# Ones-matrix products in a rounded format, and a last output block in two halves of 256 tokens

## The chip, the cores and the metric

The kernel runs on one core of one Trainium2 chip. The metric is device time in microseconds, from the first to the last instruction of the program and what lies around it. Five engines matter: TensorE (PE in the profile, its weight loads PEld), VectorE (DVE), ScalarE (ACT), GpSimd (POOL) and SyncE (SP), whose queue issues most of the transfers.

## What is computed

A trunk of two layers on 2048 tokens with 1024 channels, all float32:

```
h = rms_norm(x, norm_w);  proj = h @ w_in
branch A: gated delta rule, 4 heads, chunks, forward and backward, summed
branch B: u = cf_val * sigmoid(cf_glu); u = depthwise_conv31(u) + b
          u = silu(layer_norm(u, cf_ln_w, cf_ln_b)); y_b = (u * silu(z_b)) @ w_cf_out
y = gate_a * y_a + gate_b * y_b
x = x + y @ w_out
```

and after the second layer one more `rms_norm(x, final_norm_w)`. The change touches the norms (one value per token, which has to reach all 128 channels of a tile) and the very last output product.

## The kernel before, in words

Activations lie with channels on the 128 partitions and tokens along the free axis. A dense product of full precision is made of three products in a rounded format (`F32R`): the weight is split into a high part `whi` and a low part `wlo`, the activation into `hi` and `lo`, and for each block of 128 input channels `dense_steps` (L174 to L176) runs whi x hi, whi x lo and wlo x hi with 512 tokens moving. `split` (L157, L158) makes the two parts: ScalarE copies to the rounded format, VectorE subtracts. `weight` loads a tile of 128 output channels by two transfers of 256 KB each through two load buffers (`wraw`), and splits into a ring of two `whi` and two `wlo`.

A norm has three steps that use a 128x128 matrix of ones or the identity. `token_sum` (L200) sums squares over the channels by a product with one column of ones and leaves one sum per token, with the tokens on partitions. `rsqrt` (L190 to L196) makes the inverse root on VectorE by eleven short operations. `spread` takes these values back to a row that stands on all partitions: for each group of 128 tokens it scales the identity by the column (L206, VectorE) and multiplies by the ones (L208, TensorE), in full precision, four times for 512 tokens. Its users are the first norm (four blocks), the layer norm of branch B (`conformer_norm`, four blocks a layer), `normalise` between the layers (four) and `last_out` (four). The layer norm also needs a mean: `t` holds the sum of four channel tiles, and one product with the ones in full precision (L760) sums it over partitions. In the trace a product in full precision is two instructions.

The small temporaries come from `st`, a ring of three buffers of 512 columns. The gate evacuations (L808, `go`) use the same ring: ScalarE moves a finished tile from a TensorE bank to it, and a transfer issued by ScalarE stores it. There are three banks for dense products (`pd`) and five for the rest (`pz`).

Order of work: the convolutions and norms are Python generators that `pump` runs between dense products on credit. Each `yield` names a cost; a `yield 0.0` ends the pump of this product, so that the next step comes at least one product later; `Z` says how many such stops follow each step of the layer norm. The layer norms run during the 32 tiles of `gates(0)`. After that comes `delta`, whose instructions keep their written order, with the second half of the gates as filler. Everywhere else the framework's scheduler orders each engine's instructions by priority and by when its model has them ready, so a spread stands among the next tiles' products.

`last_out` (from L1280) ends the trunk. For each half of 1024 tokens and each block of 512 it runs eight output tiles: the product, the residual row `xr` loaded and added (L1295), the square and its sum (L222, L225, L226). Then come the token sums, the inverse root (from L1303), the spread, and eight scaled outputs (L1308), each stored by SyncE or ScalarE in turn (L1311).

Of the kernel before, what the change touches and what calls it, by code (L numbers as in the profile page):

```python
# [6 lines left out]
F32 = mybir.dt.float32  # L7
# [23 lines left out]
STEP = (5, 4, 4, 4)  # L31
TAIL = (3, 3, 3)
Z = '121'
LATE = 4
AHEAD = 4
R2 = 3.7
# [25 lines left out]
def cut(x):  # L62
    return x.rearrange("p (a i) -> p a i", a=2)
# [13 lines left out]
class Trunk:  # L77
# [79 lines left out]
        self.nc.scalar.activation(hi, src, AF.Copy)  # L157
        self.nc.vector.tensor_tensor(out=lo, in0=src, in1=hi.bitcast(F32), op=ALU.subtract)  # L158
# [39 lines left out]
    def token_sum(self, ps, src, n):  # L198
        for i in range(n):
            self.nc.tensor.matmul(ps[:, i:i + 1], src[:, i * P:(i + 1) * P], self.ones[:, 0:1],  # L200
                                  start=True, stop=True)

    def spread(self, ps, r, n):
        dg = self.pst.tile([P, NB], F32, tag="st", name="dg").rearrange("p (a b) -> p a b", b=P)
        for i in range(n):
            self.nc.vector.tensor_scalar(out=dg[:, i, :], in0=self.ident, scalar1=r[:, i:i + 1],  # L206
                                         scalar2=None, op0=ALU.mult)
            self.nc.tensor.matmul(ps[:, i * P:(i + 1) * P], self.ones, dg[:, i, :], start=True, stop=True)  # L208

    def norm_stats(self, ss):  # L210
        ps = self.pz()
# [8 lines left out]
    def add_square(self, ss, x, first):  # L220
        if first:
            self.nc.scalar.activation(ss, x, AF.Square)  # L222
        else:
            sq = self.st("sq")
            self.nc.scalar.activation(sq, x, AF.Square)  # L225
            self.nc.vector.tensor_tensor(out=ss, in0=ss, in1=sq, op=ALU.add)  # L226

# [20 lines left out]
    def run(self):  # L248
        tc, nc, a = self.tc, self.nc, self.a
        with tc.tile_pool(name="cst", bufs=1) as cst, \  # L250
                tc.tile_pool(name="vec", bufs=1) as self.pv, \
                tc.tile_pool(name="dsc", bufs=1) as self.pds, \
                tc.tile_pool(name="big", bufs=4) as self.pbig, \
                tc.tile_pool(name="mid", bufs=3) as self.pmid, \
                tc.tile_pool(name="hmd", bufs=5) as self.phm, \
                tc.tile_pool(name="stg", bufs=3) as self.pst, \
                tc.tile_pool(name="sml", bufs=14) as self.psm, \
                tc.tile_pool(name="wgt", bufs=2) as self.pw, \
                tc.tile_pool(name="drm", bufs=1, space=DRAM) as drm, \
                tc.tile_pool(name="pdn", bufs=3, space=PSUM) as self.ppd, \  # L260
                tc.tile_pool(name="pzz", bufs=5, space=PSUM) as self.ppz:
            con = cst.tile([P, 4, P], F32, name="con")
            nc.scalar.dma_start(con, a["consts"])
            self.ident = con[:, C_ID, :]
            self.ones = con[:, C_ONE, :]
# [477 lines left out]
    def conformer_norm(self, blk):  # L743
        nc = self.nc
        v_ = nc.vector
        sl = slice(blk * NB, (blk + 1) * NB)
        cv = self.mid("lnc")[:, 0:L].rearrange("p (j t) -> p j t", t=NB)
        self.load(cv, self.cv_d[:, :, sl].rearrange("j p t -> p j t"))
        zb = self.mid("lnz")[:, 0:L].rearrange("p (j t) -> p j t", t=NB)
        self.load(zb, self.zb_d[:, :, sl].rearrange("j p t -> p j t"))  # L750
        t = self.st("lnt")
        s2 = self.st("lns")
        v_.tensor_tensor(out=t, in0=cv[:, 0, :], in1=cv[:, 1, :], op=ALU.add)
        v_.tensor_tensor(out=s2, in0=cv[:, 2, :], in1=cv[:, 3, :], op=ALU.add)
        v_.tensor_tensor(out=t, in0=t, in1=s2, op=ALU.add)
        yield 1.8
        for _ in range(int(Z[0])):
            yield 0.0
        ps = self.pz()
        nc.tensor.matmul(ps, self.ones, t, start=True, stop=True)  # L760
# [25 lines left out]
        v_.tensor_tensor(out=cv, in0=cv, in1=zb, op=ALU.mult)  # L786
        self.pstore(self.u_d[:, :, sl].rearrange("j p t -> p j t"), cv)
# [492 lines left out]
    def last_out(self, l, half, xd, fnw, yhi, ylo, ahead):  # L1280
        nc, a = self.nc, self.a
        v_ = nc.vector
        for b in range(2):
            sl = slice(b * NB, (b + 1) * NB)
            tk = slice(half * HALF + b * NB, half * HALF + (b + 1) * NB)
# [3 lines left out]
            for j in range(KD):  # L1289
                next(ahead, None)  # L1290
                ps = self.pd()
                self.dense(ps, w, lambda k: (yhi[:, k, sl], ylo[:, k, sl]), KD)
                xr = self.st("xr")
                self.load(xr, xd[j][:, tk])
                v_.tensor_tensor(out=cut(xn[j]), in0=sort(ps), in1=cut(xr), op=ALU.add)  # L1295
                self.add_square(ss, xn[j], j == 0)
                if j + 1 < KD:
                    w = self.weight(a["w_out"][l, j + 1], KD)
            ps = self.pz()
            self.token_sum(ps, ss, 4)  # L1300
            v = self.sm(4, "nv")
            r = self.sm(4, "nr")
            v_.tensor_scalar(out=v, in0=ps[:, 0:4], scalar1=1.0 / D, scalar2=EPS, op0=ALU.mult, op1=ALU.add)  # L1303
            self.rsqrt(r, v, 4)
            pr = self.pz()
            self.spread(pr, r, 4)
            for j in range(KD):
                v_.scalar_tensor_tensor(out=xn[j], in0=xn[j], scalar=fnw[:, j:j + 1], in1=pr,  # L1308
                                        op0=ALU.mult, op1=ALU.mult)
                eng = nc.scalar if j % 2 else nc.sync  # L1310
                eng.dma_start(a["out"][j, :, tk], xn[j])  # L1311


def layout(inputs, depth):
# [49 lines left out]
```

## Time and profile before

| | us |
|---|---|
| median of 3 runs | 3219.36 |
| lowest, highest | 3217.04, 3219.66 |
| profiled execution | 3223.96 |
| its span | 3222.2 |

The span goes from the first to the last instruction of the profiled execution. In the lines of a timeline the first number is the start in microseconds from the span's start, the second the length of the merged row, then engine, line, operation, what it writes and reads, shape and count; in brackets the idle time of the engine before it and what ended that. In a row of a group there stand the busy time in all, the mean length of one in ns, and idle time with its releaser. A TensorE row's length includes the drain; the distance between starts tells what it holds the engine for.

### The profile page before, as it was taken

What the parts mean: (1) busy time and instruction counts of PE and PEld (TensorE: products, weight loads), DVE (VectorE), ACT (ScalarE), POOL (GpSimd) and SP (SyncE); (2) the same over time, 40 slices, a digit from 0 to 9 for tenths busy, and PEclk for the clock granted to TensorE, in tenths of its full rate; (3) what the DMA queues carried; (4) which work ended last, traced back from release to release, by engine and by line L of the source; (5) the groups of instructions that cost most, each with busy time, mean ns of one, the idle gap of its engine ahead of it and who ended that gap; (6) DMA issues with size and microseconds to landing.
All of it is one profiled execution on the core that took longest, in us unless ns stands there. A gap on an engine that the chain in (4) does not pass through costs nothing. (4 is left out here: it accounts for less than half of the span.)

```text
span 3222.2 us, 51090 instructions
## 1 busy us (share of the span) xinstructions
PE 3101.0 (96%) x19110; PEld 2711.5 (84%) x19110; DVE 2401.9 (75%) x4409; ACT 1393.5 (43%) x3104; POOL 302.2 (9%) x297
## 2 busy tenths in 40 slices
PE   6999999999999999799999999999999999989997
PEld 5788888888889998687888888888888999877786
DVE  7789898987555687645666989898955567867655
ACT  5625252522344466533345242425234445655332
POOL 3000000000022231000000000000002122200000
PEclk9999999999999999899999999999999999999999
DMA  4233232334687785654413131314358777856644
GB/s 139 88 96 94 84 100 78 102 108 132 215 289 231 261 270 174 191 187 128 141 50 107 66 116 62 119 59 122 116 188 269 236 254 246 265 155 208 206 128 147
DMA packets 427030, 501.67 MB, mean 156 GB/s; under 512 B 95712, under 2 KB 260192, under 8 KB 426784
## 3 DMA queue, kind: packets, MB, share of 16 engines
q1 hardware_dynamic: 354032, 388.58, 38.9%
q10 hardware_dynamic: 64688, 80.09, 7.1%
q0 software_dynamic: 8064, 29.76, 2.4%
q8 instruction: 150, 2.46, 0.3%
q14 instruction: 96, 0.79, 0.1%
HBM read 342.74 MB, written 155.58 MB: 155 GB/s over the span
## 5 line engine op out<-in xcount | busy, mean ns | idle before, releaser
L174 PE MATMUL pd<-h,whi 128*128 128x512 f32 x2816 | 1091.7, 388 | 0.0
L176 PE MATMUL pd<-h,wlo 128*128 128x512 f32 x2816 | 1071.3, 380 | 2.3 <-DVE wlo L158 2.3
L175 PE MATMUL pd<-h,whi 128*128 128x512 f32 x2816 | 1072.1, 381 | 0.0
L728 DVE SCALAR_TENSOR_TENSOR cacc<-gp,vec,cacc 128x1009 f32<-128x1009 f32 (+1 forms) x480 | 615.5, 1282 | 37.8 <-ACT cacc L726 34.7
L174 PEld LDWEIGHTS pd<-h,whi 128*128 128x128 f32 x2816 | 534.6, 190 | 79.3 <-issue 1.4
L176 PEld LDWEIGHTS pd<-h,wlo 128*128 128x128 f32 x2816 | 534.4, 190 | 79.5 <-DVE wlo L158 3.9
L175 PEld LDWEIGHTS pd<-h,whi 128*128 128x128 f32 x2816 | 534.5, 190 | 72.9 <-issue 1.9
L157 ACT ACTIVATE whi<-wraw 128x512 fp32r<-128x512 f32 x400 | 243.0, 624 | 488.6 <-PE pd L175 346.6
L158 DVE TENSOR_TENSOR wlo<-wraw,whi 128x512 fp32r<-128x512 f32 x400 | 279.7, 713 | 175.8 <-ACT whi L157 163.9
L553 DVE SCALAR_TENSOR_TENSOR acc<-cin,vec,acc 128x1022 f32<-128x1022 f32 (+1 forms) x192 | 246.9, 1300 | 14.7 <-ACT acc L551 13.6
L176 PE MATMUL pd<-yhi,wlo 128*128 128x512 f32 x512 | 195.3, 381 | 8.0 <-DVE wlo L158 7.9
L174 PE MATMUL pd<-yhi,whi 128*128 128x512 f32 x512 | 194.7, 380 | 1.4 <-ACT whi L157 1.3
L175 PE MATMUL pd<-ylo,whi 128*128 128x512 f32 x512 | 194.0, 379 | 0.0
L808 ACT ACTIVATE go<-pd,vec 128x512 f32<-128x512 f32 x128 | 87.0, 680 | 133.2 <-PE pd L176 122.6
L529 ACT ACTIVATE cin<-pd 128x512 f32<-128x512 f32 x96 | 57.0, 593 | 156.3 <-PE pd L176 156.1
L174 PE MATMUL pd<-gop,whi 128*128 128x512 f32 x256 | 99.9, 392 | 20.5 <-ACT gop L157 19.3
L176 PEld LDWEIGHTS pd<-yhi,wlo 128*128 128x128 f32 x512 | 96.7, 189 | 25.6 <-DVE wlo L158 12.2
L174 PE MATMUL pd<-uop,whi 128*128 128x512 f32 x256 | 102.9, 402 | 12.8 <-ACT uop L157 7.1
L1210 ACT ACTIVATE gt<-gt 128x1024 f32<-128x1024 f32 x64 | 67.6, 1058 | 108.1 <-DMA gt<-gt 98.9
L740 ACT ACTIVATE ao<-pd 128x512 f32<-128x512 f32 x64 | 38.3, 598 | 170.0 <-PE pd L176 169.9
L976 ACT ACTIVATE dm<-pz,eg 128x128 f32<-128x128 f32 x240 | 68.5, 368 | 98.8 <-PE pz L970 93.7
L174 PEld LDWEIGHTS pd<-yhi,whi 128*128 128x128 f32 x512 | 96.8, 189 | 16.4 <-ACT whi L157 3.0
(296 smaller groups left out, 4837.0 us busy)
## 6 DMA issues: line engine op xcount, KB each, us to landing
wraw<-w_in SPq DMA_DIRECT2D x240, 256.0 KB, 3.2
gt<-go ACTq DMA_DIRECT2D x128, 256.0 KB, 3.4
dl<-gr SPq DMA_DIRECT2D x128, 256.0 KB, 5.1
dl<-kq SPq DMA_DIRECT2D x64, 512.0 KB, 5.9
dl<-kv SPq DMA_DIRECT2D x64, 512.0 KB, 5.2
gt<-gt SPq DMA_DIRECT2D x64, 512.0 KB, 5.0
wraw<-w_out SPq DMA_DIRECT2D x96, 256.0 KB, 3.0
kq<-acc SPq DMA_DIRECT2D x16, 1024.0 KB, 5.5
```

The costliest lines, as they stand in the source:

```text
L157: self.nc.scalar.activation(hi, src, AF.Copy)
L158: self.nc.vector.tensor_tensor(out=lo, in0=src, in1=hi.bitcast(F32), op=ALU.subtract)
L174: mm(ps, whi[:, k, :], xhi, start=k == 0, stop=False)
L175: mm(ps, whi[:, k, :], xlo, start=False, stop=False)
L176: mm(ps, wlo[:, k, :], xhi, start=False, stop=k == kk - 1)
L529: nc.scalar.activation(cut(t[:, o + b * NB:o + (b + 1) * NB]), sort(ps), AF.Copy)
L553: self.nc.vector.scalar_tensor_tensor(out=out, in0=t[:, k:k + n], scalar=wc(k), in1=out, op0=ALU.mult, op1=ALU.add)
L728: self.nc.vector.scalar_tensor_tensor(out=acc, in0=t[:, k:k + n], scalar=wc(k), in1=acc, op0=ALU.mult, op1=ALU.add)
L740: nc.scalar.activation(cut(o), sort(ps), func)
L808: nc.scalar.activation(cut(o), sort(ps), AF.Identity, bias=self.vec[:, V_GB + j:V_GB + j + 1])
L976: nc.scalar.activation(hv(o1)[:, hd, :], pq[:, hd, :], AF.Copy, scale=eg[:, hd:hd + 1])
L1210: nc.scalar.activation(gt, gt, AF.Sigmoid)
```

## The change

It has three parts.

The ones become a tile of their own in the rounded format (`ones_r`), loaded by a separate transfer and copied by ScalarE; the old name is a view of it. `spread` splits its column of values into a high and a low part, makes two sets of scaled identities (the high ones on VectorE, the low ones on ScalarE, each in a buffer of the `st` ring) and runs two products of up to 512 columns in the rounded format that add up in one bank.

The layer norm mean splits `t` into two buffers of the `st` ring and runs two rounded products. The squares go to fresh buffers. The step's cost for `pump` is 2.5 instead of 1.8.

In the last block of the last half, only five output tiles (`PART`) run on 512 tokens. The weights of the other three are kept in a large buffer of their own; then the three tiles run on the first 256 tokens, that half is closed (sums, inverse root, spread, outputs), and the three tiles run on the other 256 tokens, which are closed in turn. In a half the last tile's squares aren't added to the sum on VectorE, but enter the token sums as a second set of products (`token_add`).

```diff
-    def weight(self, src, kk):
-        hi = self.pw.tile([P, KD, P], F32R, tag="whi", bufs=2, name="whi")[:, 0:kk, :]
-        lo = self.pw.tile([P, KD, P], F32R, tag="wlo", bufs=2, name="wlo")[:, 0:kk, :]
+    def weight(self, src, kk, kept=None):
+        if kept:
+            hi, lo = kept
...
+    def token_add(self, ps, src, n, first, last):
+        for i in range(n):
+            self.nc.tensor.matmul(ps[:, i:i + 1], src[:, i * P:(i + 1) * P], self.ones[:, 0:1],
+                                  start=first and i == 0, stop=last, skip_group_check=True)
+
     def spread(self, ps, r, n):
-        dg = self.pst.tile([P, NB], F32, tag="st", name="dg").rearrange("p (a b) -> p a b", b=P)
+        nc = self.nc
+        rh = self.psm.tile([P, 8], F32R, tag="smr", bufs=2, name="rh")
+        self.split(rh[:, 0:n], rh[:, n:2 * n], r)
+        rh = rh.bitcast(F32)
+        dg = [self.pst.tile([P, NB], F32R, tag="st", name=f"dg{i}").rearrange("p (a b) -> p a b", b=P) for i in range(2)]
         for i in range(n):
-            self.nc.vector.tensor_scalar(out=dg[:, i, :], in0=self.ident, scalar1=r[:, i:i + 1],
-                                         scalar2=None, op0=ALU.mult)
-            self.nc.tensor.matmul(ps[:, i * P:(i + 1) * P], self.ones, dg[:, i, :], start=True, stop=True)
+            nc.vector.tensor_scalar(out=dg[0][:, i, :], in0=self.ident, scalar1=rh[:, i:i + 1],
+                                    scalar2=None, op0=ALU.mult)
+            nc.scalar.activation(dg[1][:, i, :], self.ident, AF.Copy, scale=rh[:, n + i:n + i + 1])
+        for i in range(2):
+            nc.tensor.matmul(ps[:, 0:n * P], self.ones_r, dg[i][:, 0:n, :], start=i == 0, stop=i == 1)
...
+        hi = self.pst.tile([P, NB], F32R, tag="st", name="lnh")
+        lo = self.pst.tile([P, NB], F32R, tag="st", name="lnl")
+        self.split(hi, lo, t)
+        yield 2.5
...
-        nc.tensor.matmul(ps, self.ones, t, start=True, stop=True)
+        for i, part in enumerate((hi, lo)):
+            nc.tensor.matmul(ps, self.ones_r, part, start=i == 0, stop=i == 1)
+        t = self.st("lnq")
+        s2 = self.st("lnr")
...
+            whole = PART if half and b else KD
+            if whole < KD:
+                hold = self.big([P, 2, KD, NB], F32R, "wend").rearrange("p a b c -> p (a b c)")
+                parts = [hold[:, i * D:(i + 1) * D].rearrange("p (k c) -> p k c", c=P) for i in range(2 * (KD - whole))]
...
+            ws = [self.weight(a["w_out"][l, j], KD, parts[2 * (j - whole):2 * (j - whole) + 2]) for j in range(whole, KD)]
+            n = NB // 2
+            for g in (o, o + n):
+                for j, w in zip(range(whole, KD), ws):
+                    x = product(j, w, g, n)
+                    if j + 1 < KD:
+                        self.add_square(ss[:, g % NB:g % NB + n], x, False)
+                sq = self.st("sq")[:, 0:n]
+                nc.scalar.activation(sq, x, AF.Square)
+                close(g, n, sq)
```

`product` and `close` hold the same statements as the loop of `last_out` before, with a width of 512 or 256 tokens.

More of the change, by code (lines that the diff above doesn't have):

```diff
@@ L33 @@
 Z = '121'
+PART = 5
 LATE = 4
@@ L158, in split @@
         self.nc.vector.tensor_tensor(out=lo, in0=src, in1=hi.bitcast(F32), op=ALU.subtract)
-    def weight(self, src, kk):
-        hi = self.pw.tile([P, KD, P], F32R, tag="whi", bufs=2, name="whi")[:, 0:kk, :]
-        lo = self.pw.tile([P, KD, P], F32R, tag="wlo", bufs=2, name="wlo")[:, 0:kk, :]
+    def weight(self, src, kk, kept=None):
+        if kept:
+            hi, lo = kept
+        else:
+            hi = self.pw.tile([P, KD, P], F32R, tag="whi", bufs=2, name="whi")[:, 0:kk, :]
+            lo = self.pw.tile([P, KD, P], F32R, tag="wlo", bufs=2, name="wlo")[:, 0:kk, :]
         for k in range(0, kk, 4):
@@ L223, in add_square @@
         else:
-            sq = self.st("sq")
+            sq = self.st("sq")[:, 0:x.shape[1]]
             self.nc.scalar.activation(sq, x, AF.Square)
@@ L261, in run @@
                 tc.tile_pool(name="pzz", bufs=5, space=PSUM) as self.ppz:
-            con = cst.tile([P, 4, P], F32, name="con")
-            nc.scalar.dma_start(con, a["consts"])
+            con = cst.tile([P, 3, P], F32, name="con")
+            nc.scalar.dma_start(con, a["consts"][:, 0:3])
+            ones = self.st("ones")[:, 0:P]
+            nc.scalar.dma_start(ones, a["consts"][:, C_ONE])
+            self.ones_r = cst.tile([P, P], F32R, name="ones")
+            nc.scalar.activation(self.ones_r, ones, AF.Copy)
             self.ident = con[:, C_ID, :]
-            self.ones = con[:, C_ONE, :]
+            self.ones = self.ones_r.bitcast(F32)
             self.con = con
@@ L1282, in last_out, with product, close @@
         v_ = nc.vector
+        def product(j, w, o, n):
+            sl = slice(o, o + n)
+            ps = self.pd()[:, 0:n]
+            self.dense(ps, w, lambda k: (yhi[:, k, sl], ylo[:, k, sl]), KD)
+            xr = self.st("xr")[:, 0:n]
+            self.load(xr, xd[j][:, half * HALF + o:half * HALF + o + n])
+            x = xn[j][:, o % NB:o % NB + n]
+            v_.tensor_tensor(out=cut(x), in0=sort(ps), in1=cut(xr), op=ALU.add)
+            return x
+        def close(o, n, sq):
+            q = n // P
+            c = slice(o % NB, o % NB + n)
+            ps = self.pz()
+            self.token_add(ps, ss[:, c], q, True, sq is None)
+            if sq is not None:
+                self.token_add(ps, sq, q, False, True)
+            v = self.sm(q, "nv")
+            r = self.sm(q, "nr")
+            v_.tensor_scalar(out=v, in0=ps[:, 0:q], scalar1=1.0 / D, scalar2=EPS, op0=ALU.mult, op1=ALU.add)
+            self.rsqrt(r, v, q)
+            pr = self.pz()[:, 0:n]
+            self.spread(pr, r, q)
+            for j in range(KD):
+                x = xn[j][:, c]
+                v_.scalar_tensor_tensor(out=x, in0=x, scalar=fnw[:, j:j + 1], in1=pr, op0=ALU.mult, op1=ALU.mult)
+                eng = nc.scalar if j % 2 else nc.sync
+                eng.dma_start(a["out"][j, :, half * HALF + o:half * HALF + o + n], x)
@@ L1288, in last_out @@
             w = self.weight(a["w_out"][l, 0], KD)
-            for j in range(KD):
+            for j in range(whole):
                 next(ahead, None)
[L1291 to L1297, printed above, removed]
-                    w = self.weight(a["w_out"][l, j + 1], KD)
@@ L1299, in last_out @@
[L1299 to L1311, printed above, removed]
+                x = product(j, w, o, NB)
@@ new lines, in last_out @@
+                self.add_square(ss, x, j == 0)
+                if j + 1 < whole:
+                    w = self.weight(a["w_out"][l, j + 1], KD)
+            if whole == KD:
+                close(o, NB, None)
+                continue
+            ws = [self.weight(a["w_out"][l, j], KD, parts[2 * (j - whole):2 * (j - whole) + 2]) for j in range(whole, KD)]
[8 more added lines that the diff above has]
+                close(g, n, sq)
```

4 lines of the change are left out of this document (1 added, 3 removed).

## The prediction

> **What bounds the kernel now.** I read the page first, then a table of busy time by stage.
>
> ```profile
> span 3222.2 us, 51090 instructions
> PE 3101.0 (96%) x19110; PEld 2711.5 (84%) x19110; DVE 2401.9 (75%) x4409; ACT 1393.5 (43%) x3104; POOL 302.2 (9%) x297
> 80.00:1500.00 1420.00, 1379.80 (x8766) 1212.07 (x8765) 1076.23 (x1981) 621.44 (x1431) 140.04 (x138) 0.99 0.50 158
> 2900.00:3222.00 322.00, 292.67 (x1346) 247.22 (x1344) 204.31 (x360) 120.73 (x180) 0.00 (x0) 0.98 0.53 172
> ```
>
> The columns of the last two lines are stretch, length, then PE, PEld, DVE, ACT and POOL busy, granted clock, DMA share and GB/s. PE works for 97% of the long middle at a clock of 0.99. There, PE time saved is time saved, as long as no other engine makes PE wait. In the last 322 us PE works for 91%: chains through VectorE and ScalarE show.
>
> The change concerns two products with the matrix of ones: the layer norm mean (L760, 8 times) and the spread (L208, 20 times). Their rows in the timeline of PE:
>
> ```profile
> 777.42 1.02 PE L760 MATMUL pz<-lnt,con 128*128 128x512 f32 x2
> 777.88 0.78 PE L174 MATMUL pd<-h,whi 128*128 128x512 f32 x1
> 778.49 0.38 PE L175 MATMUL pd<-h,whi 128*128 128x512 f32 x1
> 778.71 0.38 PE L176 MATMUL pd<-h,wlo 128*128 128x512 f32 x1
> 794.71 1.05 PE L208 MATMUL pz<-dg,con 128*128 128x128 f32 x8
> 795.52 0.46 PE L174 MATMUL pd<-h,whi 128*128 128x512 f32 x1
> 795.82 0.38 PE L175 MATMUL pd<-h,whi 128*128 128x512 f32 x1
> ```
>
> A product in the rounded format with 512 columns starts every 0.22 us (778.49 to 778.71). From L760's start to L175 lie 1.07 us; less the one L174 between, the mean costs PE 0.85. In the same way four spreads cost 1.11 - 0.22 = 0.89, which is 0.11 for each of eight instructions, weight load and 128 columns of full precision. Both groups are queued straight behind dense products: PE waits for neither.
>
> **The change part by part.** *Layer norm.* The mean becomes two rounded products of 512 columns, 0.43 instead of 0.85: 8 x 0.42 = 3.4 us less. The spread becomes two also, 0.43 instead of 0.89: 8 x 0.46 = 3.7 less. What it adds must hide:
>
> ```profile
> 768.63 0.69 DVE L755 TENSOR_TENSOR lnt<-lnt,lns 128x512 f32<-128x512 f32 x1
> 788.84 0.69 ACT L808 ACTIVATE go<-pd,vec 128x512 f32<-128x512 f32 x1 [3.01 <-PE pd L176]
> 791.95 0.88 DVE L206 TENSOR_SCALAR dg<-con,lr 128x128 f32<-128x128 f32 x4
> 794.69 1.15 ACT L157 ACTIVATE whi<-wraw 128x512 fp32r<-128x512 f32 x2 [5.17 <-PE pd L175]
> 778.88 0.69 ACT L808 ACTIVATE go<-pd,vec 128x512 f32<-128x512 f32 x1 [2.71 <-DMA gt<-go]
> 774.96 0.69 ACT L808 ACTIVATE go<-pd,vec 128x512 f32<-128x512 f32 x1 [0.64 <-DMA gt<-go]
> L157 ACT ACTIVATE whi<-wraw 128x512 fp32r<-128x512 f32 x400 | 243.0, 624 | 488.6 <-PE pd L175 346.6
> L1210 ACT ACTIVATE gt<-gt 128x1024 f32<-128x1024 f32 x64 | 67.6, 1058 | 108.1 <-DMA gt<-gt 98.9
> ```
>
> Before the mean, one split of 512 columns: 0.62 on ScalarE and 0.69 on VectorE, 1.4 with their hand-over. The sum was ready at 769.3 and the mean ran at 777.4, so 8 us cover it. Before the spread, a split of four columns (about 0.2 on each engine, the cost of the short operations in the rows of the end below; 0.5 in all), then four scaled identities on ScalarE beside VectorE's. Between 512 and 1024 columns ScalarE's time grows by 0.43, so 128 columns take about 0.31, and, overlapping like the pair at 794.69, four take 1.0. The operand, ready at 792.8 now, comes 0.6 to 1.2 us later, by how far the parts overlap; the spread ran at 794.7, so 1.9 us cover it. ScalarE is free from 789.5 to 794.7. If that cover goes, PE stands at the spread, and with it every gate product behind it, and each evacuation that waits for those.
>
> The cost I cannot read off is buffers: the staging ring has three, spread now takes two of them and the mean briefly three, and the gate evacuations use the same ring. Two rows show an evacuation waiting for one, 2.71 and 0.64; PE does not stop, since it has three banks. Bounds: 0, and 8 x 2.71 = 21.7. I take the shorter wait once or so a layer, +1.3, as PE rode over the longer one. The mean's larger price in the planner (2.5 for 1.8) moves the norms by one gate tile; counted through the credits, the last ends three tiles ahead of the delta stage instead of four, so the fillers stay in place. Zero.
>
> *Spreads of the norms.* Layer 0's normalise has four, in pairs between dense products: 4 x 0.46 = 1.8 less. The first norm has four more:
>
> ```profile
> PE pz L200 <- DMA x<-x: 13.6, 1, 13.6
> PE pz L208 <- DVE dg L206: 7.6, 5, 2.6
> ```
>
> In these rows of the waits PE starts by standing 13.6 us for the input, which hides the ones' own small load and ScalarE copy, and the five waits for a spread's identities fall into two spreads of the first norm, one transition and the closing spread. I count zero: -1.8 if all four are kept, +1 if two chains are longer by 0.5.
>
> *Last norm, three spreads ahead of the end.* Here VectorE's chain decides:
>
> ```profile
> 3163.84 0.17 DVE L196 SCALAR_TENSOR_TENSOR nr<-rst,nr 128x4 f32<-128x4 f32 x1
> 3164.03 0.87 DVE L206 TENSOR_SCALAR dg<-con,nr 128x128 f32<-128x128 f32 x4
> 3164.32 1.15 ACT L157 ACTIVATE whi<-wraw 128x512 fp32r<-128x512 f32 x2 [4.67 <-PE pd L175]
> 3165.57 5.36 DVE L1308 SCALAR_TENSOR_TENSOR xl<-xl,fnw,pz 128x512 f32<-128x512 f32 x8 [0.67 <-PE pz L208]
> 3172.78 0.48 PE L176 MATMUL pd<-yhi,wlo 128*128 128x512 f32 x1 [1.42 <-DVE wlo L158]
> ```
>
> From the inverse root (3164.0) to L1308 pass 1.57 us, and the 5.36 us of L1308 hold back the weight split on which PE then stands for 1.42. With the split of four columns, ScalarE's 1.0 and two products with their drain the 1.57 becomes about 2.1. PE is 0.46 earlier, its weight 0.5 later: +0.5 for each of three, +1.5. Bounds: -1.4 (PE decides), and +5 (ScalarE's identities stand behind the pair at 3164.32, 1.15 more each).
>
> *The end.* The chain after the last product, and the weights ahead of it:
>
> ```profile
> 3204.56 0.38 PE L176 MATMUL pd<-yhi,wlo 128*128 128x512 f32 x1
> 3204.97 0.69 DVE L1295 TENSOR_TENSOR xl<-pd,xr 128x512 f32<-128x512 f32 x1 [3.04 <-PE pd L176]
> 3205.75 0.63 ACT L225 ACTIVATE sq<-xl 128x512 f32<-128x512 f32 x1 [4.54 <-DVE xl L1295]
> 3206.41 0.69 DVE L226 TENSOR_TENSOR ss<-ss,sq 128x512 f32<-128x512 f32 x1 [0.74 <-ACT sq L225]
> 3207.16 1.05 PE L200 MATMUL pz<-con,ss 128*128 128x1 f32 x8 [2.22 <-DVE ss L226]
> 3208.25 0.16 DVE L1303 TENSOR_SCALAR nv<-pz 128x4 f32<-128x4 f32 x1 [1.15 <-PE pz L200]
> 3210.49 0.87 DVE L206 TENSOR_SCALAR dg<-con,nr 128x128 f32<-128x128 f32 x4
> 3212.95 5.35 DVE L1308 SCALAR_TENSOR_TENSOR xl<-xl,fnw,pz 128x512 f32<-128x512 f32 x8 [1.58 <-PE pz L208]
> 3187.06 0.63 ACT L157 ACTIVATE whi<-wraw 128x512 fp32r<-128x512 f32 x1 [2.88 <-DMA wraw<-w_out]
> 3191.18 0.64 ACT L157 ACTIVATE whi<-wraw 128x512 fp32r<-128x512 f32 x1 [1.87 <-DMA wraw<-w_out]
> 3197.07 0.69 DVE L158 TENSOR_TENSOR wlo<-wraw,whi 128x512 fp32r<-128x512 f32 x1 [0.63 <-ACT whi L157]
> L206 DVE TENSOR_SCALAR dg<-con,lr 128x128 f32<-128x128 f32 x32 | 7.1, 282 | 0.5
> ```
>
> Now: add, square, sum, token sums and their drain to 3208.25, inverse root to 3210.49, spread to 3212.95, L1308 to 3218.3, the last store 3.9 more: 17.3 us after the product's end at 3204.94. With 256 columns a VectorE operation takes about 0.42 (a third of the way from 0.28 at 128 to 0.69), a ScalarE one 0.41, eight L1308 8 x 0.40. After: add 0.45, square 0.5, token sums by four instructions 0.65, inverse root 2.24, spread 1.7, L1308 3.2, the store 3.5 (half the bytes): 12.2. That is 5.0 less.
>
> Against it, PE ends later. Six half products of 24 at 0.11 (a full weight load for 256 columns, like a spread's instruction) are 16.0 instead of 15.5; twelve more token-sum instructions and one more spread 1.5; and the weights: they come every 4.1 us (3187.06, 3191.18) by two load buffers, the last split ends at 3197.76, while the first halves want all three weights by 3197.4 at the latest, ten instructions before their end: 1.5 more. Their loads now stand on SP's queue ahead of the residual loads of the same tiles, which are needed only at a product's end. The first half's closing runs on VectorE beside the second half's products; its stores, half of them on ScalarE's queue, hold the second half's squares there until about 3208, when the last product is still running. Together 3.5 later, 5.0 shorter: -1.5 (from -5 to +2).
>
> A rule speaks against the halves. The Trainium skill, TensorE: Matmul & The Clock Gate, Part 3, section The mechanism, says that weight loads overlap with running products only where the row groups differ. By that a half product would pay its load in full, and the sum would be the last rival's; the 0.11 per instruction of the spreads at 794.71, loads included, does not agree.
>
> *Sum:* -3.4 - 3.7 + 1.3 - 1.8 + 1.5 - 1.5 = -7.6. The profiled execution took 3223.96 (span 3222.2), 0.14% above the median 3219.36; I carry the difference over: 3211.8 us.
>
> **Rivals.** *All of it kept:* the three transitions follow PE (-1.4), no buffer wait, second-half products fill the weight wait at the end (-3.0): -3.4 - 3.7 - 1.8 - 1.4 - 3.0 = -13.3, 3206.1. For it: no product of the norms waits in the rows above. Against: the 1.42 behind L1308.
>
> *Swallowed:* each of the eight means and eight spreads meets the 0.64 wait on the ring, 10.2 in place of 1.3: +1.3, 3220.7. For it: the ring was already full at 774.96. Against: two such waits in that stretch did not stop PE.
>
> *Slower, buffers:* in each of the eight norms an evacuation holds ScalarE by the 2.71 of the row at 778.88 just ahead of its half of the spread, and PE stands: 21.7 in place of 1.3 gives +12.8, 3232.2. It decides once that hold exceeds the 0.7 us of cover that the spread has left at the least (1.9 less 1.2).
>
> *Half products without overlap:*
>
> ```profile
> 777.85 0.19 PEld L174 LDWEIGHTS pd<-h,whi 128*128 128x128 f32 x1 [0.24 <-issue]
> ```
>
> If this 0.19 did not hide behind 256 columns, 144 instructions would take 27 us more, 3239. The spreads' pace speaks against it. It is the rule of the Trainium skill named above.
>
> **How the numbers follow.** Forecast 0.47, all kept 0.18, swallowed 0.20, buffers 0.12, no overlap 0.03. The forecast's own range is 3207 to 3217, mostly from the transitions and the end. The range for 8 in 10 is 3205 to 3222: it takes in both neighbours and leaves out the slower rivals. A measurement of this kernel tells about 0.2%, 6.4 us, from no change: faster means below 3212.9. The forecast lies just under it, so 0.6 of its chance and all of "all kept" count as faster, 0.46; the rest of it and "swallowed" as the same, 0.39; the two others as slower, 0.15.
>
> **What would show it.** Right: the mean and the spread as two rows of 512 columns that hold PE for 0.43; no new wait of PE on ScalarE's identities between 760 and 890; L1308 of the three transitions about 0.5 later after the inverse root; PE's last product about 3.5 us later relative to the block's start, and 12.2 us from it to the end. Wrong: PE waiting at L760 or the spread by a microsecond or more in the gates stage, half products pacing well over 0.11, a closing chain over 14 us, or other stages moving because the order of instructions changed.

## The result, and the profile after

The changed kernel takes 3267.15 us (median of 4 runs, 3265.03 to 3269.88) where the kernel before took 3218.20 beside it (3216.25 to 3219.66): a ratio of 1.0153, interval 1.0135 to 1.0171. It is 49 us slower. 3211.8 was forecast, and 3267 lies outside the range and past the dearest rival.

The page of the changed kernel begins:

```profile
span 3264.9 us, 51212 instructions
PE 3109.3 (95%) x19072; PEld 2711.7 (83%) x19072; DVE 2412.6 (74%) x4462; ACT 1428.2 (44%) x3217; POOL 303.4 (9%) x297
```

PE is busy for 8 us more and the span is 43 us longer: TensorE did not get more work, it stands. To find where, I cut both spans at the same events: the stretch from a layer's first gate evacuation (`go`, L808 before, L833 after) to its first product of `delta`, which holds the four layer norms, for both layers; and the last block's products from the first to the last. The table of busy time by stage, columns as in the prediction, for the kernel before:

```profile
715.50:904.00 188.50, 184.96 (x878) 160.20 (x879) 119.23 (x200) 65.00 (x111) 13.64 (x15) 0.99 0.56 188
2292.90:2478.30 185.40, 183.21 (x877) 158.95 (x878) 120.70 (x200) 65.04 (x111) 13.54 (x15) 1.00 0.58 191
2930.60:3204.50 273.90, 260.88 (x1200) 220.36 (x1199) 167.31 (x289) 99.65 (x151) 0.00 (x0) 1.00 0.53 173
```

and for the changed kernel:

```profile
715.70:921.80 206.10, 189.28 (x850) 162.43 (x849) 123.26 (x207) 73.92 (x135) 12.87 (x14) 0.95 0.51 170
2303.00:2510.10 207.10, 190.25 (x850) 163.52 (x851) 123.67 (x208) 73.76 (x135) 12.68 (x14) 0.94 0.50 166
2965.40:3247.80 282.40, 264.54 (x1265) 223.85 (x1263) 172.49 (x317) 104.73 (x171) 0.00 (x0) 0.99 0.52 170
```

The layer norm stretches are 17.6 and 21.7 longer, 39.3 of the 42.7 us between the spans. The last products are 8.5 longer; what lies between the stretches makes up the rest (-7.7 between the two norm stretches, +3.0 ahead of the last products, -0.6 behind them, +0.2 ahead of all). The granted clock fell from 0.99 and 1.00 to 0.95 and 0.94 in the norm stretches, and in the last products only from 1.00 to 0.99.

What TensorE waits for, by the view of waits (the row of the spread before stands in the prediction); the columns are us in all, times, longest. Before:

```profile
PE pz L200 <- DVE lnt L766: 5.7, 4, 2.0
```

After:

```profile
PE pz L204 <- DVE lnq L791: 32.2, 6, 5.7
PE pz L223 <- DVE dg L219: 11.2, 8, 4.1
```

The token sums of six of the eight norms stand for over 5 us each until VectorE has added the squares. Of the spread's 11.2 us only 0.2 lie in the two norm stretches. VectorE is not the cause. ScalarE's timeline at the first of the six:

```profile
809.01 0.69 ACT L833 ACTIVATE go<-pd,vec 128x512 f32<-128x512 f32 x1 [1.39 <-DVE lnl L159]
809.73 0.33 ACTq L152 DMA_DIRECT2D gt<-go  x1
811.90 0.63 ACT L788 ACTIVATE lnq<-lnc 128x512 f32<-128x512 f32 x1 [2.20 <-DVE lnc L786]
812.44 0.61 ACT L790 ACTIVATE lnr<-lnc 128x512 f32<-128x512 f32 x1
818.25 0.69 ACT L833 ACTIVATE go<-pd,vec 128x512 f32<-128x512 f32 x1 [5.20 <-DMA gt<-go]
819.39 0.63 ACT L790 ACTIVATE lnr<-lnc 128x512 f32<-128x512 f32 x1 [0.45 <-ACT go L833]
```

Of four squares two are done at 813.05. The third, at 819.39, could have run from 813.8 on, when VectorE's first sum (813.08, 0.69 long) had freed its buffer, but ahead of it in ScalarE's order stands a gate evacuation, which waits 5.20 us for a buffer of the staging ring: the three hold `lnq`, `lnr` and the `go` of 809.01, whose store, issued at 809.73, ends that wait. In the five other norms the evacuation at the same step waits 5.08 to 5.63. VectorE's timeline shows the sum of squares behind it:

```profile
820.05 0.69 DVE L791 TENSOR_TENSOR lnq<-lnq,lnr 128x512 f32<-128x512 f32 x1 [6.28 <-ACT lnr L790]
```

and TensorE's, first at a norm without the wait, the token sums that stand ahead of its next dense products:

```profile
793.69 0.95 PE L204 MATMUL pz<-ones,lnq 128*128 128x1 f32 x8
794.50 0.46 PE L178 MATMUL pd<-h,whi 128*128 128x512 f32 x1
...
822.19 1.87 PE L204 MATMUL pz<-ones,lnq 128*128 128x1 f32 x8 [5.31 <-DVE lnq L791]
823.92 0.77 PE L178 MATMUL pd<-h,whi 128*128 128x512 f32 x1
824.48 0.63 PE L179 MATMUL pd<-h,whi 128*128 128x512 f32 x1
...
827.90 0.47 PE L178 MATMUL pd<-h,whi 128*128 128x512 f32 x1
```

A stall costs more than itself. The token sums take 1.73 us (822.19 to 823.92) where those of the first norm took 0.81 (793.69 to 794.50). Then eight products start 0.43 apart (824.48 to 827.90) instead of 0.22, and 0.56 passes ahead of them instead of 0.22: 2.0 more. So one stall adds 0.9 + 2.0 = 2.9 of slow clock. The granted clock was 0.50 from 822.19 to 828.00. Worked out in the same way, the six stalls add 2.4 to 3.9 each, 2.9 in the mean.

The sum over both layers: token sums wait 32.2 - 5.7 = 26.5 longer; six times 2.9 is 17.4; the shorter means and spreads give back 8 x 0.81 = 6.5 (0.39 each for the mean, 0.42 for the spread, rows below). That makes 37.4 of the 39.3 measured. The rest, and slow stretches that the kernel before has too, I have not assigned.

The Trainium skill, TensorE: Matmul & The Clock Gate, Part 1, What's actually happening, says that the array drops to half its clock after an idle window of about 3.4 us and gets the full one back after as long a busy one. The stall of 5.31 agrees, and the slow stretch behind it, 5.7 us from 822.19 to 827.90, is longer than the page's window. But half pace can follow a shorter wait, as TensorE's timeline of the kernel before shows:

```profile
862.70 1.05 PE L200 MATMUL pz<-con,lnt 128*128 128x1 f32 x8 [1.54 <-DVE lnt L766]
...
864.93 0.63 PE L176 MATMUL pd<-h,wlo 128*128 128x512 f32 x1
...
867.92 0.43 PE L174 MATMUL pd<-h,whi 128*128 128x512 f32 x1
```

After a wait of 1.54 us the token sums and four products run at full pace, and then seven products take 2.99 (864.93 to 867.92), 0.43 each; the granted clock was 0.51 from 864.60 to 868.10. The three other waits for token sums in that kernel (2.00, 0.60 and 1.59) have no such stretch behind them, so these traces give no length of wait from which it comes.

In ScalarE's own waits there is one row for this ring. Before:

```profile
ACT go L808 <- DMA gt<-go: 6.7, 3, 3.3
```

After:

```profile
ACT go L833 <- DMA gt<-go: 47.8, 14, 5.6
```

### The profile page after: what moved, and what is told of

It reads as the page before. It is cut to its first block, busy times and chain, and to the rows that moved or that the text cites. A ratio compares the mean times of both kernels' runs of the same rounds, so it can differ in the third digit from the quotient of the medians.

```text
span 3264.9 us, 51212 instructions
## 1 busy us (share of the span) xinstructions
PE 3109.3 (95%) x19072; PEld 2711.7 (83%) x19072; DVE 2412.6 (74%) x4462; ACT 1428.2 (44%) x3217; POOL 303.4 (9%) x297
## 5 line engine op out<-in xcount | busy, mean ns | idle before, releaser
L159 DVE TENSOR_TENSOR wlo<-wraw,whi 128x512 fp32r<-128x512 f32 x394 | 273.0, 706 | 160.5 <-ACT whi L158 141.3
L180 PE MATMUL pd<-yhi,wlo 128*128 128x512 f32 x488 | 186.8, 383 | 9.4 <-DVE wlo L159 9.3
L178 PE MATMUL pd<-yhi,whi 128*128 128x512 f32 x488 | 186.2, 382 | 2.5 <-ACT whi L158 2.5
L179 PE MATMUL pd<-ylo,whi 128*128 128x512 f32 x488 | 185.7, 380 | 0.0
L833 ACT ACTIVATE go<-pd,vec 128x512 f32<-128x512 f32 x128 | 87.4, 683 | 163.6 <-PE pd L180 102.8
L178 PE MATMUL pd<-uop,whi 128*128 128x512 f32 x256 | 102.4, 400 | 12.2 <-ACT uop L158 7.2
L178 PEld LDWEIGHTS pd<-yhi,whi 128*128 128x128 f32 x488 | 92.7, 190 | 17.4 <-ACT whi L158 4.6
```

What stands on the lines that cost most here:

```text
L178: mm(ps, whi[:, k, :], xhi, start=k == 0, stop=False)
L179: mm(ps, whi[:, k, :], xlo, start=False, stop=False)
L180: mm(ps, wlo[:, k, :], xhi, start=False, stop=k == kk - 1)
L833: nc.scalar.activation(cut(o), sort(ps), AF.Identity, bias=self.vec[:, V_GB + j:V_GB + j + 1])
```

## The experiments

The theory to test: the mean's two parts and the fresh buffers for the squares fill the ring, an evacuation between the squares waits for a store, and the token sums wait for that. Rivals: the step cost of 2.5 only moved the norm under a badly placed evacuation; the longer chain of mean and spread does it by itself, with any buffers; or one of the three parts alone carries the loss.

Each run is compared with the kernel before in its own session; that kernel's medians were 3222.03, 3218.82 and 3219.69. Where the expectations count runs, the second is the mean in a wide buffer, the fourth the halves alone, and the fifth the one that moves the spread's identities too.

### The place: the old step cost

```diff
-        yield 2.5
+        yield 1.8
```

> The changed kernel with the planner's cost of the mean's step back at 1.8. Buffers: the ring of three is what holds ScalarE between the squares, wherever the step stands, so PE still stands 5 us or so at the token sums of six layer norms, and the time stays within 8 us of the changed kernel's 3267. Place: the dearer step moved the norms by one gate tile and so onto the large loads; with 1.8 the six waits go back to the four short ones of before, and the time falls by 25 to 35 us, to 3232 to 3242.

Measured: 3267.94, ratio 1.0149 (1.0134 to 1.0164), as the changed kernel's 1.0153. The cost does nothing; that rival is out. The prediction's zero for it holds.

### The parts one by one

The spread alone (kernel before, with `ones_r` and the new `spread`):

```diff
-            self.nc.tensor.matmul(ps[:, i * P:(i + 1) * P], self.ones, dg[:, i, :], start=True, stop=True)
+            nc.scalar.activation(dg[1][:, i, :], self.ident, AF.Copy, scale=rh[:, n + i:n + i + 1])
+        for i in range(2):
+            nc.tensor.matmul(ps[:, 0:n * P], self.ones_r, dg[i][:, 0:n, :], start=i == 0, stop=i == 1)
```

> The kernel before with the new spread alone (rounded ones, two products, two buffers). Buffers, if the spread's second buffer were to blame: 3230 to 3245, with waits at the layer norms. If the mean's buffers or place are to blame: the spread keeps its saving of 0.46 on PE in the middle and gives some back at the last norm, 3212 to 3222.

Measured: 3222.05, ratio 1.0003 (0.9994 to 1.0013). No difference, where the prediction's terms for the spreads came to -4.0 (-3.7 - 1.8 + 1.5). In its waits ScalarE stands for the ring five times as long as in the kernel before:

```profile
ACT go L818 <- DMA gt<-go: 33.1, 10, 5.1
```

So ScalarE stood for 33 us, and the run lost at most what the spreads were to save. What counts is what stands behind the wait in ScalarE's order. The longest of these waits comes behind all four squares, the last of which ended at 836.5:

```profile
841.59 0.69 ACT L818 ACTIVATE go<-pd,vec 128x512 f32<-128x512 f32 x1 [5.05 <-DMA gt<-go]
```

The mean alone (kernel before, with `ones_r`, the mean in two products, and fresh buffers for the squares):

```diff
-        nc.tensor.matmul(ps, self.ones, t, start=True, stop=True)
+        for i, part in enumerate((hi, lo)):
+            nc.tensor.matmul(ps, self.ones_r, part, start=i == 0, stop=i == 1)
+        t = self.st("lnq")
+        s2 = self.st("lnr")
```

> The kernel before with the mean alone as two rounded products, its two more buffers and fresh buffers for the squares. Buffers of the mean: the waits at the token sums come with it alone, 5 to 6 us in six norms less four old waits: 3240 to 3252. If it needs the spread's second buffer as well, no more than 3228.

Measured: 3235.04, ratio 1.0046 (1.0029 to 1.0064), about 16 us slower. That is between the two outcomes expected, and the waits are at another place: TensorE's longest row of the norms is now the spread, 23.0 where it was 7.6:

```profile
PE pz L208 <- DVE dg L206: 23.0, 9, 6.3
```

ScalarE's timeline at the first layer's second norm:

```profile
817.51 0.69 ACT L818 ACTIVATE go<-pd,vec 128x512 f32<-128x512 f32 x1 [4.13 <-DMA gt<-go]
...
818.65 0.63 ACT L157 ACTIVATE whi<-wraw 128x512 fp32r<-128x512 f32 x1 [0.46 <-ACT go L818]
```

and VectorE's:

```profile
819.31 0.69 DVE L158 TENSOR_TENSOR wlo<-wraw,whi 128x512 fp32r<-128x512 f32 x1 [2.67 <-ACT whi L157]
```

The evacuation that waits came behind the four squares here, but ahead of a weight split. VectorE has the other half of that split in the middle of the inverse root (816.48 to 819.92), and the spread's identities stand behind the root. It is the same wait by another way, and a third of the loss.

The fresh buffers alone (kernel before, with these two lines behind its full-precision mean):

```diff
+        t = self.st("lnq")
+        s2 = self.st("lnr")
```

> The kernel before, with nothing but fresh buffers of the ring of three for the squares after the mean, and the mean in full precision. If the taking of buffers anew is what lets a gate evacuation between the squares, it alone costs 15 to 35 us: 3233 to 3253. If the number of buffers held at once (three at the split) is needed for it, the time stays within 5 us of before.

Measured: 3229.56, ratio 1.0027 (1.0017 to 1.0038), about 11 us slower for two allocations and no arithmetic, again between the two outcomes expected. Its token sums wait twice as long as in the kernel before (5.7):

```profile
PE pz L200 <- DVE lnq L768: 11.2, 4, 3.8
```

The halves alone (kernel before, with the last block's two halves):

> The kernel before with the last block in halves alone. The prediction's sum for it: -1.5, between -5 and +2, so 3213 to 3220; the changed kernel's last products end 8.5 us later than the stage before them moved, so if that is the halves' doing it gives 3222 to 3228 instead.

Measured: 3220.82, ratio 1.0007 (0.9996 to 1.0017). No difference. So the parts alone cost 16, 0 and 0, and together 49: they share something.

### The ring, emptied from one side

The mean's parts moved to the pool of large buffers, the squares in the old ones:

```diff
-        hi = self.pst.tile([P, NB], F32R, tag="st", name="lnh")
-        lo = self.pst.tile([P, NB], F32R, tag="st", name="lnl")
+        both = self.phm.tile([P, 1072], F32R, tag="hm", name="lnb")
+        hi, lo = both[:, 0:NB], both[:, NB:2 * NB]
...
-        t = self.st("lnq")
-        s2 = self.st("lnr")
```

> The changed kernel with the two parts of the mean in one wide buffer of another ring, and the squares in the old two buffers, cost 2.5 kept. Buffers: the squares no longer take buffers anew, the evacuation keeps its place after them, the six waits of 5.6 us at the token sums go: 3230 to 3242. Place: nothing of where the norms stand is changed: 3260 to 3270.

Measured: 3238.52, ratio 1.0060 (1.0043 to 1.0078). Beside the 3267.94 of the run with the old cost, in the same session, 29 us are gone, with the same arithmetic and the same chain. The rival of the longer chain can hold at most what is left, 16.5 over the kernel before.

The spread's two sets of identities moved as well (both sets in one large buffer for the layer norms):

```diff
+        if wide:
+            both = self.phm.tile([P, 1072], F32R, tag="hm", name="dgw")
+            dg = [both[:, i * NB:(i + 1) * NB].rearrange("p (a b) -> p a b", b=P) for i in range(2)]
...
-        self.spread(pr, r, 4)
+        self.spread(pr, r, 4, True)
```

> The changed kernel with the mean's two parts and the layer norm's two sets of identities each in one wide buffer of another ring, squares in the old two buffers: the layer norms take no more of the ring of three than before. Buffers: the layer norms then save on PE what the prediction said, 3.4 + 3.7 less at most; what is left is the last norm and the halves, which in the second run ended 6 us later than before, so 3216 to 3226. If something other than the ring holds the norms back (the splits and identities themselves on ScalarE), it stays at the second run's 3233 to 3240.

Measured: 3248.57, ratio 1.0090 (1.0070 to 1.0109), 30 over the kernel before where the last run was 16.5 over it: a miss. ScalarE's evacuations hardly wait for the ring any more (3.4 us in all), and yet TensorE stands at the spread. Its waits:

```profile
PE pz L227 <- DVE dgw L223: 27.0, 8, 7.1
```

VectorE's timeline at one of them:

```profile
855.01 0.69 DVE L776 TENSOR_TENSOR lnt<-lnc 128x512 f32<-128x512 f32 x1 [3.92 <-DMA lnc<-cv]
...
858.98 0.87 DVE L223 TENSOR_SCALAR dgw<-con,rh 128x128 fp32r<-128x128 f32 x4
```

The same thing on another engine: in the middle of the inverse root (847.35 to 858.6), behind a weight split that waits 2.74 us, the next norm's first sum stands in VectorE's order and waits 3.92 us for its input; root, identities and spread wait with it. Another allocation gave another order, and the order put a wait for a transfer ahead of the step on which TensorE hung.

### The ring, emptied from the other side

The changed kernel with the gate evacuations of the first half in large buffers. The mean, the spread and the squares keep the ring:

```diff
-            o = self.st("go")
+            o = self.st("go") if half else self.hm("gw")[:, 0:NB]
```

> The changed kernel with the gate evacuations of the layer norms' stage in the wide ring, so that the norms have the three small buffers to themselves. Evacuations waiting for a buffer: nothing on ScalarE waits between the squares any more, the six waits of 5.6 us at the token sums go, and PE waits for the norms' products 10 us or less in both layers; what is left is the last norm and the halves: 3222 to 3236. If late loads, which hold the next norm's first sum on VectorE ahead of this norm's chain as in the fifth run, are the common cause: still 3240 to 3255.

Measured: 3232.03, ratio 1.0039 (1.0026 to 1.0053): 12 us over the kernel before in place of 49, by one line. The profiled execution took 3223.56, the lowest of its times. The norm stretches of it, in the table by stage:

```profile
713.00:899.50 186.50, 181.73 (x846) 156.08 (x844) 125.57 (x199) 73.81 (x135) 13.47 (x16) 1.00 0.55 187
2282.40:2471.80 189.40, 182.55 (x846) 156.06 (x844) 125.81 (x199) 73.70 (x135) 13.40 (x16) 1.00 0.55 185
```

They are 19.6 and 17.7 shorter than in the changed kernel, and the clock is back at 1.00. No gate evacuation waits for a store, the four squares run through (809.56 to 813.48), and the row of token sums that wait for `lnq` is gone. ScalarE's timeline, the evacuation ahead of the squares and the last square:

```profile
808.98 0.69 ACT L833 ACTIVATE gw<-pd,vec 128x512 f32<-128x512 f32 x1 [3.54 <-PE pd L180]
...
812.85 0.63 ACT L790 ACTIVATE lnr<-lnc 128x512 f32<-128x512 f32 x1 [0.76 <-DVE lnq L791]
```

This is the mechanism of the result. One wait that is left shows below, under "All that helped, together". The profile is that of the fastest of nine executions (to 3243.24), so where the 12 us of the median lie isn't shown.

Is the wide buffer a gain of its own? The kernel before with the same line:

> The kernel before with only the gate evacuations of that stage in the wide ring. If the four waits at its token sums (5.7 us) come from evacuations that wait for a buffer too, they go: 3211 to 3217. If they are the norm's own chain, the time is that of before, 3217 to 3222.

Measured: 3222.59, ratio 1.0005 (0.9996 to 1.0014). No: in the kernel before the three rows of 6.7 us cost nothing.

### Why the store comes late

From its issue at 809.73 to the evacuation that it lets go at 818.25 pass 8.5 us; the page gives 3.6 as the median of such a store. Just ahead of it SyncE issued a load of 1 MB (`zb`, at 808.40), and GpSimd a store of 1 MB (`u`, at 808.67). The changed kernel with the load allocated and issued after the inverse root:

```diff
-        zb = self.mid("lnz")[:, 0:L].rearrange("p (j t) -> p j t", t=NB)
-        self.load(zb, self.zb_d[:, :, sl].rearrange("j p t -> p j t"))
...
+            zb = self.mid("lnz")[:, 0:L].rearrange("p (j t) -> p j t", t=NB)
+            self.load(zb, self.zb_d[:, :, sl].rearrange("j p t -> p j t"))
```

> The changed kernel with the norm's second 1 MB load (the gate rows zb) issued after the token sums instead of with the first. In the changed kernel an evacuation's store that runs beside that load landed 8.5 us after its issue. If the load is what makes the store late, the store lands in 3 to 5 us, the six waits fall from 5.6 us to 2 or less, and the time falls by 12 to 25: 3242 to 3255. If stores are late for another reason: 3262 to 3270.

Measured: 3268.27, ratio 1.0148 (1.0134 to 1.0162). Nothing changed. ScalarE's timeline in its profile:

```profile
821.03 0.69 ACT L833 ACTIVATE go<-pd,vec 128x512 f32<-128x512 f32 x1 [5.42 <-DMA gt<-go]
```

But the load's place didn't change either: it goes out at 810.97 on SyncE's queue, 1.3 us ahead of the store at 812.30, as before the edit (808.40 and 809.73). In both it follows the end of the norm ahead's last use of its buffer (L811, which ends at 810.94 and 808.37). So the experiment did not make the difference that it was meant to make. GpSimd's store, which goes out 1.06 us ahead of the evacuation's in both, is a rival that no run separates, and why the store takes 8.5 us stays open.

### The end

The halves alone, with the residual rows of the three tiles loaded ahead into a buffer of their own:

```diff
+            rows = self.mid("xrw")[:, 0:(KD - whole) * NB].rearrange("p (k c) -> p k c", c=NB)
+            for j in range(whole, KD):
+                self.load(rows[:, j - whole, :], xd[j][:, half * HALF + o:half * HALF + o + NB])
```

> The kernel before with the last block in halves alone, as in the fourth run, but with the residual rows of the three tiles loaded ahead into a buffer of their own, not behind the first half's stores on SP's queue. The second half's closing should then start when its products end: about 3.5 us less than the fourth run (3217 for its 3221) and a chain from the last product to the end of 13 us instead of 15.5. If the stores are not what holds it, no change.

Measured: 3217.87, ratio 0.9996 (0.9984 to 1.0007). It answers to the end of the changed kernel. There SyncE's queue has:

```profile
3244.55 2.68 SPq L1336 DMA_DIRECT2D out<-xl  x4
3247.33 1.69 SPq L146 DMA_DIRECT2D xr<-x  x2
```

VectorE's timeline:

```profile
3250.52 0.42 DVE L1316 TENSOR_TENSOR xl<-pd,xr 128x256 f32<-128x256 f32 x1 [1.86 <-DMA xr<-x]
```

and TensorE's last products:

```profile
3247.64 0.28 PE L179 MATMUL pd<-ylo,wend 128*128 128x256 f32 x1
3247.75 0.28 PE L180 MATMUL pd<-yhi,wend 128*128 128x256 f32 x1
```

The residual loads of the second half stand behind the first half's stores on SyncE's queue and come late; from the last product's end (3247.75 + 0.28) to the span's end are 16.9 us. With the rows ahead the last product is:

```profile
3201.70 0.28 PE L180 MATMUL pd<-yhi,wend 128*128 128x256 f32 x1
```

Its span is 3214.1: 12.1 us from the last product's end. But its last products take 279.3 us (2922.4 to 3201.7) where the kernel before takes 273.9, so what the chain gives (about 5) the products take (5.4).

### All that helped, together

The changed kernel with wide evacuations, the new spread in the layer norms and `normalise` only, and the residual rows ahead:

> The parts that the runs leave standing: gate evacuations in the wide ring, the mean as two products, the new spread in the layer norms and between the layers only (the old one in the first and the last norm), and the halves with their residual rows loaded ahead. If the ring was what the change lost by, the prediction's savings come through: 3.4 + 3.7 + 1.8 on PE and 1 to 3 at the end, 3205 to 3213. If order on VectorE and late loads take them back, 3218 to 3235.

Measured: 3223.15, ratio 1.0007 (0.9998 to 1.0016). No gain over the kernel before. One wait takes the shorter mean back: TensorE stands for the mean's first part six times, 7.7 us in all; with the wide evacuations alone it is 7.4, and there I followed it. VectorE's timeline of the kernel with wide evacuations alone, at the third norm's mean:

```profile
825.78 0.69 DVE L774 TENSOR_TENSOR lnt<-lnt,lns 128x512 f32<-128x512 f32 x1
828.90 2.29 DVE L811 TENSOR_TENSOR lnc<-lnc,lnz 128x2048 f32<-128x2048 f32 x1 [2.44 <-ACT lnc L809]
831.11 0.69 DVE L159 TENSOR_TENSOR lnl<-lnt,lnh 128x512 fp32r<-128x512 f32 x1
```

ScalarE's:

```profile
828.78 0.61 ACT L158 ACTIVATE lnh<-lnt 128x512 fp32r<-128x512 f32 x1
```

and TensorE's:

```profile
829.45 0.50 PE L783 MATMUL pz<-lnh,ones 128*128 128x512 f32 x1 [1.93 <-ACT lnh L158]
...
831.95 0.41 PE L783 MATMUL pz<-lnl,ones 128*128 128x512 f32 x1
```

The sum is there at 826.5. Its high part stands on ScalarE behind the norm ahead (L809, which runs from 825.95 for 2.93 us), its low part on VectorE behind L811 (2.29 us). TensorE stands for 1.93, and the second product comes 5.5 us after the sum. Six of the eight means wait, four of them for 1.5 us or more; those 7.4 are more than the 3.4 that the shorter mean was to save. No run has the rest of this kernel with the old mean, and what took the other savings isn't shown.

## Why the prediction was wrong, by its own steps

**The step that failed** is the price of the buffers: "I take the shorter wait once or so a layer, +1.3, as PE rode over the longer one." Evacuations waited 47.8 us for the ring in the changed kernel, 6.7 before, and where +1.3 stood TensorE lost 43.9: 26.5 more of waits at the token sums and 17.4 of slow clock behind them. What I took from the row of 2.71 was that TensorE has three banks to ride on, and so that the evacuation itself can be late. That can hold: the spread alone has 33.1 us of such waits and is no slower than before. What it leaves out is that ScalarE works in order, and everything behind the waiting evacuation waits too. The wait of 2.71 stood ahead of all four squares, and the first of them, at 780.80, still waited 1.24 for VectorE after it; in the changed kernel the wait stands between the second and the third square. Of the signs named for the gates stage, a wait of a microsecond or more at the mean or the spread, neither came (at most 0.2 at a time); no sign named the token sums.

**The rival of the buffers** had this kind of mechanism, an evacuation that holds ScalarE until TensorE stands. It had the wrong place and size: eight times 2.71 ahead of the spread, where the runs show six times over 5 us ahead of the token sums, and 2.9 of slow clock behind each, which no term had. I did not put the same wait ahead of the other ScalarE steps of the norm, though the squares are four of them, with VectorE and TensorE behind each. And its bound, 21.7, was no bound: it took the 2.71 of one of two rows, where the kernel before has three with a longest of 3.3, and from a ring with fewer users.

**The cover of the mean** failed too: "The sum was ready at 769.3 and the mean ran at 777.4, so 8 us cover it." Those rows are the first norm's, with no norm ahead. In the others the split queues behind the norm ahead on both engines, and with the ring out of the way TensorE still waits 7.4 us for it. Where four norms follow each other, the cover has to be read at the second.

**Holds of the products** were right. TensorE's timeline of the changed kernel at a spread:

```profile
799.76 0.63 PE L223 MATMUL pz<-dg,ones 128*128 128x512 f32 x2
800.23 0.38 PE L178 MATMUL pd<-h,whi 128*128 128x512 f32 x1
```

0.47 for the spread, and in the same way 0.46 for the mean (782.87 to 783.33), where 0.43 was predicted. It shows in no run's time; at the mean the operands come later.

**The planner's cost** at zero was right: with 1.8 the time is the same.

**The spreads between the layers**, -1.8, can't be told: the stretch between the norms of the two layers is 1386.6 with the spread alone (905.1 to 2291.7), 1388.9 before, and moves by as much in kernels that leave it as it was (1384.7 with fresh buffers alone, 907.8 to 2292.5).

**The three transitions** were sized too small. ScalarE's timeline at one of them:

```profile
3202.52 1.28 ACT L221 ACTIVATE dg<-con,rh 128x128 fp32r<-128x128 f32 x4 [0.23 <-DVE rh L159]
```

and TensorE's:

```profile
3211.59 0.48 PE L180 MATMUL pd<-yhi,wlo 128*128 128x512 f32 x1 [2.50 <-DVE wlo L159]
```

From the end of the root (3202.05) to L1334 (3204.39) pass 2.3 us where 2.1 was predicted and 1.57 was, with ScalarE's four identities 1.28 (predicted 1.0); TensorE's wait behind it grew from 1.42 to 2.50. That is +1.1, not +0.5, at this transition and at the first; at the second TensorE waits 2.21 once, where it waited 1.13 and 1.10 before. The spread alone makes the last products 276.1 us long (2927.3 to 3203.4), 2.2 more than before, where +1.5 stood.

**The end.** The half products pace at 0.11 (3247.64 to 3247.75), as predicted, so the last rival falls. The chain was to shorten from 17.3 to 12.2 and took 16.9, since "which are needed only at a product's end" was right for each load and wrong for the queue they stand on; with the loads ahead it took 12.1. TensorE's later end was predicted as 3.5 and came to 4.1 with the halves alone (278.0, 2923.1 to 3201.1). With the chain mended the halves change nothing that can be measured. So without any wait for the ring the change would still have been no gain: -7.6 was forecast, and the kernel that frees the ring is slower than before by 0.39% (0.26 to 0.53).

## What to carry to other kernels

Before you put a temporary into a shared ring, list who else takes from it, and look at each taker that frees its buffer only by a transfer: the price of its wait is not that instruction but all that stands behind it in its engine's order, and then what the bounding engine has queued behind that. Price such a wait by the step that it would stand ahead of, at the worst place, and read cover at a repetition in the middle of a row of stages, not at the first. When a change loses far more than its arithmetic could, give one user of the ring other buffers: one line told here what a sum over rows had not.

## What the runs showed of the hardware that was not expected

- A stall of TensorE of 5.3 us was followed by 5.7 us at half pace (822.19 to 827.90), which adds 2.9 us; one of 1.54 us was followed, four products later, by 3.0 us of it (864.93 to 867.92), and one of 2.00 us (837.53) by none.
- A store of 256 KB that lands in 3.6 us in the median released its buffer 8.5 us after its issue at this step (809.73 to 818.25); the cause wasn't found.
- Four scaled identities of 128x128 take ScalarE 1.28 us, where I had taken 1.0 from the growth between 512 and 1024 columns.
